# Linear recurrence layer on 128-channel tiles, with block gates that read rows of neighbouring tiles

## The chip, the cores and the metric

The kernel runs on one core of one Trainium2 chip. The metric is device time in microseconds (us) of one execution of the whole kernel, the median of several runs. The kernel computes four layers; the change concerns the second one alone, the linear recurrence layer (rglru in the code).

## The reference

A layer normalises two streams, 256 context rows and 512 latent rows of 1024 channels, applies a mixer, and adds the gated result to the streams. The mixer of the second layer is this, cut to what matters (LRU_WIDTH is 1408, in 16 blocks of 88 channels):

```python
def block_diag(x, w, b):
    xb = x.reshape(B, T, LRU_BLOCKS, LRU_BLOCK_DIM)
    return jnp.einsum('btnc,ncd->btnd', xb, w).reshape(B, T, LRU_WIDTH) + b

def rglru_coeffs(x, p, d):
    r = jax.nn.sigmoid(block_diag(x, p['gate_w'][d, 0], p['gate_b'][d, 0]))
    i = jax.nn.sigmoid(block_diag(x, p['gate_w'][d, 1], p['gate_b'][d, 1]))
    log_a = -LRU_C * r * jax.nn.softplus(-p['lam'][d])
    a = jnp.exp(log_a)
    b = jnp.sqrt(-jnp.expm1(2.0 * log_a)) * (i * x)
    return a, b

def rglru_mixer(h_l, h_c, p, ctx_out):
    def pre(h):
        z = h @ p['w_in']
        xr, g = z[..., :LRU_WIDTH], z[..., LRU_WIDTH:]
        return depthwise_conv_centred(xr, p['conv_w'], p['conv_b']), jax.nn.silu(g)
    ...
    for d in range(2):
        a, b = rglru_coeffs(x_c, p, d)
        hc, hc_final = linear_scan(a, b, h0, rev)
        a, b = rglru_coeffs(x_l, p, d)
        hl, _ = linear_scan(a, b, hc_final, rev)
    out_l = ((hs_l[0] + hs_l[1]) * g_l) @ p['w_out']
```

The gates r and i of a channel depend on the 88 channels of its own block only. Blocks of 88 do not line up with tiles of 128: 1408 is 16 blocks or 11 tiles.

## The kernel before

Channels lie on partitions and the 768 tokens (256 + 512) along the free dimension. Every product in fp32 is made of three matmuls on operands split into a rounded high part and a remainder (`split` at L224, `load_w` at L208): high by high, low by high, high by low. Each of the three is two instructions, one of 256 and one of 512 columns, which is called a pair here.

**Projections.** `dense` (L1392) makes one 128-channel tile of the input projection: 8 slices of the 1024 inputs, 24 pairs. There are 11 tiles x and 11 tiles g, in the order of L1387. A tile's weights are loaded and split one tile ahead: at slice 2 the generator calls `ahead` (L1397), which issues the DMA, the high cast (here on ScalarE and VectorE in turn, `HL`), and the subtraction of the remainder on VectorE (L221). After an x tile, `xtile` copies PSUM to `xf` on ScalarE (L1412), does the four-tap convolution on VectorE (L1415, L1417) and moves the rows by DMA into tiles of 88 channels, `xb` (L1424, L1425). After a g tile, `gtile` computes silu (L1445, L1446).

**Gates and recurrence.** `pair` (L1461) takes two blocks of 88. For each of two directions d, a key is one (block, direction), so that a pair has four. `pair_in` splits the inputs `xb` and the gate weights, VectorE and GpSimd sharing it. Each of eight gate outputs is three pairs of matmuls (L1476) and a sigmoid on ScalarE (L1480). Then ScalarE runs a burst over the four keys: four tanh (L1485), four exp (L1489), four sqrt (L1492), with table loads between. Then VectorE runs two elementwise operations (L1498, L1499) and the scan (L1501 forwards, L1504 and L1505 backwards) for each key, GpSimd adds the two directions (L1506), DMAs carry the sum from 88-channel tiles back to 128-channel tiles `zt` (L1513), VectorE multiplies by the gate g (L1517) and a DMA writes the tile to DRAM (L1519).

**Order.** `merge` (L130) interleaves two generators by weights, the projections and the pairs. ScalarE keeps the order in which the program is written (`manual_schedule`, L1530), so there an instruction waits for all that is written ahead of it. The orders of the other engines are set when the kernel is built; on the chip each engine takes its instructions in that order. After the layer, `out_proj` (L373) loads the 11 tiles back and starts its matmuls (L244).

```python
            merge(projs(), 160.0 + XP, [(pairs(), 22.0 * 8)])
```

Of the kernel before, what the change touches and what calls it, by code (L numbers as in the profile page):

```python
# [10 lines left out]
F32 = mybir.dt.float32  # L11
F32R = mybir.dt.float32r
# [137 lines left out]
class Build:  # L150
# [1195 lines left out]
    LRU_LAM, LRU_GB = 55, 87  # L1346

    def rglru(self, li, pv, md, xs, acc, xsp, last):
        tc, nc, a = self.tc, self.nc, self.a
        B = 88  # L1350
        NB = 16
        self.hi_dve = HL
        toks = [(0, TC), (TC, TL)]
        self.open(dict(h=16, xf=2, sq=2), wb=(2, 2, 2))

        lam = pv[0:B, self.LRU_LAM:self.LRU_LAM + 32]
        st = lambda n: self.gp.tile([P, 32], F32, tag=n, name=self.nm(n), bufs=1)[0:B, :]
        ab, u, s, s2, t, spl = st("sa"), st("su"), st("ss_"), st("s2"), st("st"), st("spl")
        spn = self.gp.tile([P, 32], F32, tag="spn", name=self.nm("spn"), bufs=1)[0:B, :]
# [44 lines left out]
        def xtile(m):  # L1404

            for outs in dense(m):
                yield 1.0
            xp = self.g("xf")
            for z in (0, 258, 772):
                nc.gpsimd.memset(xp[:, z:z + 2], 0.0)  # L1410
            for pt, o0, n in ((outs[0], 2, TC), (outs[1], 260, TL)):
                nc.scalar.copy(xp[:, o0:o0 + n], pt[:, :n])  # L1412
            xc = self.g("sq")
            cw = lambda j: pv[:, self.LRU_CW + j * 11 + m:self.LRU_CW + j * 11 + m + 1]
            nc.vector.tensor_scalar(xc[:, 2:772], xp[:, 0:770], cw(0), pv[:, self.LRU_CB + m:self.LRU_CB + m + 1], op0=ALU.mult, op1=ALU.add)  # L1415
            for j in range(1, 4):
                nc.vector.scalar_tensor_tensor(out=xc[:, 2:772], in0=xp[:, j:j + 770], scalar=cw(j), in1=xc[:, 2:772], op0=ALU.mult, op1=ALU.add)  # L1417
            for b in range(NB):
                lo, hi = max(m * P, b * B), min((m + 1) * P, (b + 1) * B)
                if lo >= hi:  # L1420
                    continue
                if b not in xb:
                    xb[b] = self.g("xb")
                nc.sync.dma_start(xb[b][lo - b * B:hi - b * B, 0:TC], xc[lo - m * P:hi - m * P, 2:2 + TC])  # L1424
                nc.sync.dma_start(xb[b][lo - b * B:hi - b * B, TC:T], xc[lo - m * P:hi - m * P, 260:260 + TL])  # L1425
# [34 lines left out]

        def pair(p):  # L1461

            self.mark(f"pair{p}")
            bl = (2 * p, 2 * p + 1)
            keys = [(b, d) for b in bl for d in range(2)]
# [4 lines left out]
            for gi, dstt in ((0, R), (1, I)):  # L1470
                for b, d in keys:
                    c0 = (d * 2 + gi) * B
                    outs = [self.psb(), self.psb()]
                    for p_i, (wt, xt) in enumerate(((W[b][0], X[b][0]), (W[b][1], X[b][0]), (W[b][0], X[b][1]))):
                        for pt, (s0, n) in zip(outs, SEGS):
                            nc.tensor.matmul(pt[:B, :n], wt[:B, c0:c0 + B], xt[:B, s0:s0 + n], start=(p_i == 0), stop=(p_i == 2))  # L1476
                    o = dstt[b, d] = self.g("sg")
                    cb = self.LRU_GB + (d * 2 + gi) * NB + b
                    for pt, (s0, n) in zip(outs, toks):
                        nc.scalar.activation(o[:B, s0:s0 + n], pt[:B, :n], AF.Sigmoid, bias=pv[0:B, cb:cb + 1])  # L1480
                    yield 1.0

            for b, d in keys:
                A[b, d] = self.g("aa")
                nc.scalar.activation(A[b, d][:B, :T], R[b, d][:B, :T], AF.Tanh, scale=spl[:, d * NB + b:d * NB + b + 1])  # L1485
# [440 lines left out]
```

## Time and profile before

| | |
|---|---|
| median of 3 runs | 3079.63 us (3076.31 to 3083.82) |
| the profiled execution, its own time | 3069.68 us |
| its span in the trace | 3067.8 us |
| mean granted TensorE clock in it | 0.905 |
| matmuls of the layer's projections and gates | 1056 and 384 |
| first projection matmul of the layer | 1070.61 us |
| last gate matmul starts | 1398 us |
| first matmul of the output projection | 1446.29 us |

Times in the trace are counted from the span's start. TensorE is PE, VectorE is DVE, ScalarE is ACT, GpSimd is POOL, and SP is the queue that issues the DMAs. "Idle before" is the time in which an engine had nothing running ahead of the instruction, and the releaser is what ended it. A clock of 1.00 is 2.4 GHz, 0.50 is 1.2 GHz.

### The profile page before, as it was taken

The numbers are of one execution on the slowest core, as the hardware profiler recorded it, in microseconds if no ns is written. First come the engines' busy times: TensorE is split into PE (matmuls) and PEld (weight loads), VectorE is DVE, ScalarE is ACT, GpSimd is POOL, SyncE is SP. The second block draws the span as 40 slices with busy tenths as digits, with TensorE's granted clock in tenths as the row PEclk, the third lists the DMA queues.
The fourth block names the chain that finished last, engine by engine and source line by source line (L and its number), as shares of the span: only waits on it lengthen the run. The fifth ranks groups of instructions, "written<-read, shape, count | busy, mean of one in ns | idle before, by whom it ended". The sixth has DMA issues, their size and how long they took to land. (4 is left out here: it accounts for less than half of the span.)

```text
span 3067.8 us, 66309 instructions
## 1 busy us (share of the span) xinstructions
PE 2639.3 (86%) x27760; PEld 2146.5 (70%) x27760; DVE 2009.2 (65%) x3325; ACT 1462.7 (48%) x2666; POOL 759.9 (25%) x640
## 2 busy tenths in 40 slices
PE   5999988888887988883989999998897887888887
PEld 3876777677776777762778888877684665777775
DVE  4768787697873478896334344343778777888853
ACT  3454553556553266664243443442454444656561
POOL 1013442031212034643022232220104333111211
PEclk9998899899998999895989999999797888889988
DMA  6235544444326422222731111046234545533423
GB/s 222 93 119 191 185 174 157 138 133 131 111 88 218 171 67 80 88 68 101 265 110 47 49 47 56 28 153 222 67 105 177 182 170 176 153 122 122 132 72 117
DMA packets 169552, 391.84 MB, mean 128 GB/s; under 512 B 20518, under 2 KB 52262, under 8 KB 169254
## 3 DMA queue, kind: packets, MB, share of 16 engines
q1 hardware_dynamic: 169254, 387.61, 37.9%
q8 instruction: 218, 3.57, 0.5%
q14 instruction: 80, 0.66, 0.1%
HBM read 281.24 MB, written 97.65 MB: 124 GB/s over the span
## 5 line engine op out<-in xcount | busy, mean ns | idle before, releaser
L634 PE MATMUL pa<-x,wh 128*128 128x512 f32 (+1 forms) x1552 | 408.2, 371 | 43.3 <-ACT x L227 24.0
L634 PEld LDWEIGHTS pa<-x,wh 128*128 128x128 f32 x1552 | 288.1, 202 | 98.8 <-ACT x L227 28.6
L244 PE MATMUL pa<-z,wh 128*128 128x256 f32 (+1 forms) x992 | 243.4, 357 | 62.0 <-ACT z L227 57.6
L1574 PE MATMUL pa<-h,wh 128*128 128x256 f32 (+1 forms) x1024 | 255.6, 355 | 8.0 <-ACT wh L218 7.0
L244 PEld LDWEIGHTS pa<-z,wh 128*128 128x128 f32 x992 | 173.0, 193 | 105.1 <-ACT z L227 59.0
L221 DVE TENSOR_TENSOR wl<-wr,wh 128x1024 fp32r<-128x1024 f32 (+1 forms) x148 | 190.6, 1290 | 81.2 <-ACT wh L218 80.5
L634 PE MATMUL pa<-x,wl 128*128 128x512 f32 (+1 forms) x776 | 232.5, 370 | 6.0 <-DVE wl L221 6.0
L218 ACT CAST wh<-wr 128x1024 fp32r<-128x1024 f32 (+1 forms) x137 | 146.5, 1070 | 190.9 <-PE pa L244 126.1
L912 DVE TENSOR_TENSOR tmpN<-al,N 128x31 f32<-128x31 f32 (+15 forms) x496 | 211.9, 427 | 14.0
L914 DVE TENSOR_TENSOR N<-N,tmpN 128x31 f32<-128x31 f32 (+15 forms) x496 | 210.6, 425 | 12.8
L1574 PEld LDWEIGHTS pa<-h,wh 128*128 128x128 f32 x1024 | 179.0, 194 | 45.3 <-issue 17.6
L1401 PE MATMUL pa<-h,wh 128*128 128x256 f32 x704 | 169.5, 352 | 17.2 <-DVE gt L1446 9.3
L634 PEld LDWEIGHTS pa<-x,wl 128*128 128x128 f32 x776 | 156.5, 204 | 31.4 <-DVE wl L221 7.9
L1401 PEld LDWEIGHTS pa<-h,wh 128*128 128x128 f32 x704 | 129.0, 198 | 38.5 <-issue 5.6
L407 DVE SCALAR_TENSOR_TENSOR x<-pa,md,x 128x512 f32<-128x512 f32 (+1 forms) x56 | 33.4, 632 | 167.5 <-PE pa L244 167.5
L244 PE MATMUL pa<-z,wl 128*128 128x256 f32 (+1 forms) x496 | 138.6, 351 | 0.5 <-DVE wl L221 0.5
L227 ACT CAST x<-xf 128x770 fp32r<-128x770 f32 x96 | 80.1, 835 | 123.0 <-DVE xf L528 73.6
L854 PE MATMUL A<-krs,be 64*128 64x128 f32 x1536 | 120.2, 295 | 19.6 <-ACT sc L865 8.8
L1574 PE MATMUL pa<-h,wl 128*128 128x256 f32 (+1 forms) x512 | 136.2, 346 | 0.6 <-DVE wl L221 0.6
L733 POOL TENSOR_SCALAR pcs<-pm 128x12 f32<-128x12 f32 (+2 forms) x48 | 38.4, 812 | 387.2 <-ACT pm L730 374.7
L868 DVE TENSOR_TENSOR sc<-A,msk 128x512 f32<-128x512 f32 x128 | 82.7, 685 | 74.3 <-PE A L854 74.1
L854 PEld LDWEIGHTS A<-krs,be 64*128 64x128 f32 x1536 | 101.4, 196 | 34.9 <-ACT sc L865 9.5
(329 smaller groups left out, 6592.6 us busy)
## 6 DMA issues: line engine op xcount, KB each, us to landing
wr<-in_l_win_dram SPq DMA_DIRECT2D x118, 512.0 KB
ar<-in_l_ada_dram SPq DMA_DIRECT2D x88, 512.0 KB
krd<-kr SPq DMA_DIRECT2D x32, 768.0 KB
bed<-be SPq DMA_DIRECT2D x32, 768.0 KB
krs<-krd SPq DMA_DIRECT2D x96, 256.0 KB
be<-bed SPq DMA_DIRECT2D x96, 256.0 KB
kr<-krd SPq DMA_DIRECT2D x96, 256.0 KB
uv<-vn SPq DMA_DIRECT2D x192, 64.0 KB
```

The costliest lines, as they stand in the source:

```text
L218: nc.scalar.copy(hi, raw)
L221: lo_eng.tensor_tensor(out=lo, in0=raw, in1=hi.bitcast(F32), op=ALU.subtract)
L227: nc.scalar.copy(hi, src)
L244: nc.tensor.matmul(outs[si][:mw, :n], wt[:kp, ws], xt[:kp, s0:s0 + n], start=(kt == 0 and p_i == 0), stop=(kt == nk - 1 and p_i == 2),)
L634: nc.tensor.matmul(outs[si][:, :n], wt[:, ws], xt[:, s0:s0 + n], start=(first and p_i == 0), stop=(final and p_i == 2))
L733: nc.gpsimd.tensor_scalar(pcs[:, m, o0:o0 + iv.shape[1], d], iv, 1.0, None, op0=ALU.mult)
L854: nc.tensor.matmul(T_["s"][hh][:, c * 128:c * 128 + 128].rearrange("p (s x) -> p s x", s=2), T_["be"][hs, c, :], kv, start=True, stop=True)
L868: y = op("V", 602, pr, [x], lambda h, ov2=ov2, mv=mv, iv=iv: nc.vector.tensor_tensor(out=ov2, in0=iv().rearrange("p (j q x) -> p j q x", j ...
L912: nc.vector.tensor_tensor(out=tv, in0=al[:, i + 1:32, i:i + 1].broadcast_to([P, n, w]), in1=N[:, i:i + 1, 0:w].broadcast_to([P, n, w]), op ...
L914: nc.vector.tensor_tensor(out=N[:, i + 1:32, 0:w], in0=N[:, i + 1:32, 0:w], in1=tv, op=ALU.subtract))
L1401: nc.tensor.matmul(pt[:, :n], wt[:, ws], xt[:, s0:s0 + n], start=(kt == 0 and p_i == 0), stop=(kt == KT - 1 and p_i == 2))
L1574: nc.tensor.matmul(pt[:, :n], wt[:, ws], xt[:, s0:s0 + n], start=(kt == 0 and p_i == 0), stop=(kt == KT - 1 and p_i == 2))
```

## The change

All of the layer works on 11 tiles of 128 channels. The convolved x stays in its tile `xc` (five buffers) and is split there. The gates of an output tile m are a matmul over whole 128-row sources with zero-padded weights: an odd tile reads itself and one gathered tile of the neighbours' edge rows (`halo`, moved by two DMAs and split into `ha`); an even tile reads itself and its neighbours whole. So gate outputs cost two or three times three pairs. The zero-padded weights are loaded one (tile, gate) ahead by `gw_in`. `unit` takes two tiles, four keys as before. The moves to 88-channel tiles and back are gone. All weight casts are on ScalarE, the order of the projections and the merge weights are new. Line numbers of the new kernel are about 1 to 13 higher: L1413 for the copies, L1416 and L1418 for the convolution, L1465 for the gate weights, L1486 for the gate matmuls, L1492 for the sigmoids, L1497, L1502, L1505 for tanh, exp, sqrt, L1509, L1510 for the elementwise steps, L1512, L1515, L1516 for the scans, L1518 for the sum, L1519 for the gate product.

```diff
-        B = 88
-        NB = 16
-        self.hi_dve = HL
+        NT = 11
+        HSEG = ((2, TC), (260, TL))
-        self.open(dict(h=16, xf=2, sq=2), wb=(2, 2, 2))
+        self.open(dict(h=16, xf=2, xc=5, sq="xc"), wb=(3, 2, 2))
...
         def xtile(m):
...
-            xc = self.g("sq")
+            x = xc[m] = self.g("xc")
...
-            for b in range(NB):
...
-                nc.sync.dma_start(xb[b][lo - b * B:hi - b * B, 0:TC], xc[lo - m * P:hi - m * P, 2:2 + TC])
-                nc.sync.dma_start(xb[b][lo - b * B:hi - b * B, TC:T], xc[lo - m * P:hi - m * P, 260:260 + TL])
+            hi, lo = X[m] = self.g("xh", F32R), self.g("xh", F32R)
+            self.split(x[:, 2:772], hi[:, 2:772], lo[:, 2:772])
+            if m and m % 2 == 0:
+                r1, r2 = halo(m - 1)
+                n, xf = r1 + r2, self.g("xf")
+                nc.sync.dma_start(xf[0:r1, 2:772], xc[m - 2][P - r1:P, 2:772])
+                nc.sync.dma_start(xf[r1:n, 2:772], x[0:r2, 2:772])
+                hi, lo = X["n", m - 1] = self.g("ha", F32R), self.g("ha", F32R)
+                self.split(xf[:n, 2:772], hi[:n, 2:772], lo[:n, 2:772])
...
-        self.open(dict(xb=6, zt=3, gt=4, b=4, sg=12, aa=4))
+        self.open(dict(xh=8, ha=2, gt=4, sg=12, aa=4))
...
+        def gw_in(i):
+            if i < 2 * NT:
+                m, gi = divmod(i, 2)
+                n = (base[m + 1] - base[m]) * 256
+                gr = self.wp.tile([P, 768], F32, tag="wr", name=self.nm("gr"), bufs=self.wb[0])
...
+                for s_ in range(base[m + 1] - base[m]):
+                    nc.sync.dma_start(gr[:, s_ * 256:s_ * 256 + 256], a[f"l{li}_gw"][base[m] + s_, gi])
+                self.split(gr[:, :n], gh[:, :n], gl[:, :n])
+                GW[i] = gh, gl
+        def unit(ms):
+            keys = [(m, d) for m in ms for d in range(2)]
...
+                    gh, gl = GW.pop(2 * m + gi)
+                    for d in range(2):
+                        outs = [self.psb(), self.psb()]
+                        for si, (key, k) in enumerate(srcs):
+                            ws = slice(si * 256 + d * 128, si * 256 + d * 128 + 128)
+                            for p_i, (wt, xt) in enumerate(((gh, X[key][0]), (gl, X[key][0]), (gh, X[key][1]))):
+                                for pt, (s0, n) in zip(outs, HSEG):
+                                    nc.tensor.matmul(pt[:, :n], wt[:k, ws], xt[:k, s0:s0 + n], start=(si == 0 and p_i == 0), stop=(si == len(srcs) - 1 and p_i == 2))
+                        if d == 0:
+                            gw_in(2 * m + gi + 1)
+                        o = dstt[m, d] = self.g("sg")
...
+                    z = I[m, 0]
+                    nc.gpsimd.tensor_tensor(out=z[:, :T], in0=z[:, :T], in1=hs[:, :T], op=ALU.add)
+                    nc.vector.tensor_tensor(out=z[:, :T], in0=z[:, :T], in1=gt[m][:, :T], op=ALU.mult)
+                    nc.sync.dma_start(dd, z[:, :T])
...
-            merge(projs(), 160.0 + XP, [(pairs(), 22.0 * 8)])
+            merge(projs(), 160.0, [(units(), 104.0 + 25.8) + LRF])
...
+def gate_src(m):
+    out = [(m, P)]
+    if m % 2:
+        out.append((("n", m), sum(halo(m))))
+    else:
+        out += [(q, P) for q in (m - 1, m + 1) if 0 <= q < 11]
+    return out
...
-XP = 28
+LRO = "x0 x1 x2 g0 x3 g1 x4 g2 x5 g3 x6 g4 x7 g5 x8 g6 x9 g7 x10 g8 g9 g10"
+LRF = (0.10, 1.10)
-HL = (1, 2)
```

How the instructions stand at three places. The first is ScalarE behind a burst. In the kernel before, behind the four sqrt of a pair:

```order
L1492 ACTIVATE aa_13138<-aa_13138 88x768
L1412 COPY xf_13173<-pa_13097 128x256
L1412 COPY xf_13173<-pa_13098 128x512
L218 CAST wh_13205<-wr_13203 128x1024
L1480 ACT_TABLE_LOAD
L1480 ACTIVATE sg_13301<-pb_13293,pv_87 88x256
```

Now, behind the four sqrt of the unit of tiles 2 and 3; `gh_13290` is the second gate weight of tile 4, `xf_13300` and `xc_13306` belong to x tile 6, `ha_13318` is the gathered edge of tile 5, `wh_13338` the weight of x tile 7:

```order
L1505 ACTIVATE aa_13211<-aa_13211 128x768
L227 CAST gh_13290<-gr_13289 128x768
L1492 ACT_TABLE_LOAD
L1492 ACTIVATE sg_13297<-pb_13269,pv_87 128x256
L1492 ACTIVATE sg_13297<-pb_13270,pv_87 128x512
L1413 COPY xf_13300<-pa_13167 128x256
L1413 COPY xf_13300<-pa_13168 128x512
L227 CAST xh_13311<-xc_13306 128x770
L227 CAST ha_13318<-xf_13315 48x770
L218 CAST wh_13338<-wr_13336 128x1024
L1492 ACTIVATE sg_13374<-pb_13354,pv_87 128x256
```

The casts of the convolved tile and of the gathered edge now stand on ScalarE, between the copies and the next weight cast. The second place is VectorE in the same stretch, in the new kernel, from the product of tile 2 on (nine rows of the unit's elementwise work, first L1509, stand ahead of these):

```order
L1519 TENSOR_TENSOR sg_12934<-sg_12934,gt_12894 128x768
L1512 SCALAR_TENSOR_TENSOR sg_13130<-sg_13052,aa_13201 128x768
L1509 SCALAR_TENSOR_TENSOR aa_13211<-sg_13087,aa_13211 128x768
L230 TENSOR_TENSOR glo_13291<-gr_13289,gh_13290 128x768
L1510 TENSOR_TENSOR aa_13211<-aa_13211,sg_13159 128x768
L1416 TENSOR_SCALAR xc_13306<-xf_13300,pv_87 128x770
L1515 SCALAR_TENSOR_TENSOR sg_13159<-sg_13087,aa_13211 128x256
L1418 SCALAR_TENSOR_TENSOR xc_13306<-xf_13300,pv_87,xc_13306 128x770
L1516 SCALAR_TENSOR_TENSOR sg_13159<-sg_13087,sg_13159,aa_13211 128x512
L1418 SCALAR_TENSOR_TENSOR xc_13306<-xf_13300,pv_87,xc_13306 128x770
L1519 TENSOR_TENSOR sg_13130<-sg_13130,gt_13162 128x768
L1418 SCALAR_TENSOR_TENSOR xc_13306<-xf_13300,pv_87,xc_13306 128x770
```

The convolution of x tile 6 stands among the last of the unit's elementwise work; the subtractions for `xh`, `ha` and then for the weight of x tile 7 follow it. The third place is TensorE, in the new kernel, at the first matmuls of x tile 7, ahead of which stand x tile 6, g tile 4 and three gate outputs of tile 4:

```order
L1486 MATMUL pb_13401<-xh_13020,gh_13290 128x256
L1486 MATMUL pb_13402<-xh_13020,gh_13290 128x512
L1402 MATMUL pa_13436<-h_11960,wh_13338 128x256
L1402 MATMUL pa_13437<-h_11960,wh_13338 128x512
L1486 MATMUL pb_13462<-xh_12754,gh_13290 128x256
L1486 MATMUL pb_13463<-xh_12754,gh_13290 128x512
L1402 MATMUL pa_13436<-h_11960,wl_13339 128x256
L1402 MATMUL pa_13437<-h_11960,wl_13339 128x512
```

From there the projection of x tile 7 and the rest of the unit's gates alternate, so that what waits for `wh_13338` holds up both.

## Rows read from the trace of the kernel before

**Rows 1.** The page: busy time, share of the span and instructions of each engine.
```profile
PE 2639.3 (86%) x27760; PEld 2146.5 (70%) x27760; DVE 2009.2 (65%) x3325; ACT 1462.7 (48%) x2666; POOL 759.9 (25%) x640
```

**Rows 2.** Busy time of each engine in the layer's opening, body and end.
```profile
core 0: us, PE busy (x) PEld busy (x) DVE busy (x) ACT busy (x) POOL busy (x), PEclk, DMA share, GB/s
1070.60:1105.30 34.70, 29.57 (x144) 23.42 (x144) 27.22 (x51) 17.83 (x26) 10.41 (x18) 0.93 0.23 71
1105.30:1398.80 293.50, 252.66 (x1296) 206.75 (x1296) 252.53 (x233) 188.19 (x282) 144.68 (x79) 0.90 0.24 72
1398.80:1446.30 47.50, 0.04 (x2) 0.01 (x1) 27.77 (x25) 17.00 (x20) 11.69 (x5) 0.50 0.29 104
```

**Rows 3.** Timeline of PE: start us, us, instructions, idle before and releaser.
```profile
1172.32 1.01 PE L1401 MATMUL pa<-h,wl 128*128 128x256 f32 x2 [7.23 <-DVE wl L221]
...
1176.97 1.17 PE L1401 MATMUL pa<-h,wh 128*128 128x256 f32 x4
...
1224.32 0.85 PE L1401 MATMUL pa<-h,wh 128*128 128x256 f32 x4
...
1225.35 0.86 PE L1401 MATMUL pa<-h,wh 128*128 128x256 f32 x4
...
1236.04 1.58 PE L1476 MATMUL pb<-b,gh 88*88 88x256 f32 x4 [4.73 <-POOL b L230]
...
1245.74 0.93 PE L1401 MATMUL pa<-h,wh 128*128 128x256 f32 x4
```

**Rows 4.** Timeline of ACT and of DVE around one burst.
```profile
1205.35 3.42 ACT L1485 ACTIVATE aa<-sg,spl 88x768 f32<-88x768 f32 x4
...
1217.76 0.83 ACT L1412 COPY xf<-pa 128x256 f32<-128x256 f32 x2
1218.49 1.06 ACT L218 CAST wh<-wr 128x1024 fp32r<-128x1024 f32 x1
...
1221.46 1.05 ACT L1480 ACTIVATE sg<-pb,pv 88x256 f32<-88x256 f32 x2 [0.62 <-PE pb L1476]
...
1215.68 1.82 DVE L1498 SCALAR_TENSOR_TENSOR aa<-sg,aa 88x768 f32<-88x768 f32 x2 [4.21 <-ACT aa L1492]
...
1219.16 0.67 DVE L1415 TENSOR_SCALAR sq<-xf,pv 128x770 f32<-128x770 f32 x1
1219.75 1.21 DVE L221 TENSOR_TENSOR wl<-wr,wh 128x1024 fp32r<-128x1024 f32 x1
```

**Rows 5.** Single lines of the code: duration in ns, min/median/max, first and last start.
```profile
L1498 DVE SCALAR_TENSOR_TENSOR aa<-sg,aa x32: 923/948/2593, 1132.6 to 1421.5; 88x768 f32<-88x768 f32 x32
...
L1499 DVE TENSOR_TENSOR aa<-aa,sg x32: 921/944/2542, 1135.4 to 1424.1; 88x768 f32<-88x768 f32 x32
...
L1501 DVE TENSOR_TENSOR_SCAN sg<-sg,aa x16: 1739/1744/3366, 1138.2 to 1422.4; 88x768 f32<-88x768 f32 x16
...
L1504 DVE TENSOR_TENSOR_SCAN sg<-sg,aa x16: 657/676/2262, 1139.9 to 1426.6; 88x256 f32<-88x256 f32 x16
...
L1505 DVE TENSOR_TENSOR_SCAN sg<-sg,sg,aa x16: 1268/1270/1280, 1141.3 to 1429.3; 88x512 f32<-88x512 f32 x16
...
L1506 POOL TENSOR_TENSOR sg<-sg,sg x16: 1797/3148/7552, 1142.7 to 1430.7; 88x768 f32<-88x768 f32 x16
...
L1517 DVE TENSOR_TENSOR zt<-zt,gt x11: 941/959/2603, 1161.0 to 1436.3; 128x768 f32<-128x768 f32 x11
...
L1417 DVE SCALAR_TENSOR_TENSOR sq<-xf,pv,sq x33: 986/1010/2606, 1096.6 to 1371.1; 128x770 f32<-128x770 f32 x33
```

**Rows 6.** Timeline of SP and DVE: a move of rows, and the cast behind it.
```profile
1377.55 0.81 SPq L1425 DMA_DIRECT2D xb<-sq  x1
...
1380.92 1.81 DVE L229 CAST b<-xb 88x768 fp32r<-88x768 f32 x1 [0.25 <-DMA xb<-sq]
```

**Rows 7.** Timeline of DVE and PE at the layer's end.
```profile
1436.32 0.96 DVE L1517 TENSOR_TENSOR zt<-zt,gt 128x768 f32<-128x768 f32 x1 [5.78 <-DMA zt<-sg]
...
1446.29 1.01 PE L244 MATMUL pa<-z,wh 128*128 128x256 f32 x2 [47.46 <-ACT z L227]
```

More of the change, by code (lines that the diff above doesn't have):

```diff
@@ L1386, in rglru @@
         self.pq = tc.alloc_tile_pool(name=f"lps{li}", bufs=4, space=bass.MemoryType.PSUM)
-        order = [(c[0], int(c[1:])) for c in "x0 x1 x2 g0 x3 x4 g1 g2 g3 x5 x6 g4 x7 g5 x8 g6 g7 x9 g8 x10 g9 g10".split()]
-        self.plan([(a[f"l{li}_win"][m + 11 * (c == "g")], 1024) for c, m in order])
+        order = [(c[0], int(c[1:])) for c in LRO.split()]
+        self.plan([(a[f"l{li}_win"][m + NT * (c == "g")], 1024) for c, m in order])
         self.ahead(2)
-        xb, gt, zt, zs = {}, {}, {}, []
+        xc, gt, zs = {}, {}, []
+        X = {}
         def dense(m):
@@ L1461, in pair @@
[L1461 to L1465, printed above, removed]
-            R, I, A = {}, {}, {}
-            if p == 0:
-                pair_in(0)
-            yield 1.0
[L1470 to L1485, printed above, removed]
-                (nc.gpsimd if d else nc.vector).tensor_tensor(out=I[b, d][:B, :T], in0=I[b, d][:B, :T], in1=xb[b][:B, :T], op=ALU.mult)
-                yield 0.75
-            for b, d in keys:
-                nc.scalar.activation(R[b, d][:B, :T], R[b, d][:B, :T], AF.Exp, scale=spn[:, d * NB + b:d * NB + b + 1])
-                yield 0.75
-            for b, d in keys:
-                nc.scalar.activation(A[b, d][:B, :T], A[b, d][:B, :T], AF.Sqrt)
-            yield 3.0
-            if p + 1 < NB // 2:
-                pair_in(p + 1)
-            for b, d in keys:
-                aa, bb, hs = R[b, d], A[b, d], I[b, d]
-                nc.vector.scalar_tensor_tensor(out=bb[:B, :T], in0=aa[:B, :T], scalar=1.0, in1=bb[:B, :T], op0=ALU.add, op1=ALU.mult)
-                nc.vector.tensor_tensor(out=bb[:B, :T], in0=bb[:B, :T], in1=hs[:B, :T], op=ALU.mult)
@@ L1506, in pair @@
-                    nc.gpsimd.tensor_tensor(out=I[b, 0][:B, :T], in0=I[b, 0][:B, :T], in1=hs[:B, :T], op=ALU.add)
-                    for m in range(11):
-                        lo_, hi_ = max(m * P, b * B), min((m + 1) * P, (b + 1) * B)
-                        if lo_ >= hi_:
-                            continue
-                        if m not in zt:
-                            zt[m] = self.g("zt")
-                        nc.sync.dma_start(zt[m][lo_ - m * P:hi_ - m * P, 0:T], I[b, 0][lo_ - b * B:hi_ - b * B, 0:T])
@@ L1514, in pair @@
[L1514 to L1517 removed]
+                    nc.vector.tensor_tensor_scan(out=rv(hs, TC, TL), data0=rv(aa, TC, TL), data1=rv(bb, TC, TL), initial=hs[:, 0:1], op0=ALU.mult, op1=ALU.add)
+                    z = I[m, 0]
+                    nc.gpsimd.tensor_tensor(out=z[:, :T], in0=z[:, :T], in1=hs[:, :T], op=ALU.add)
@@ L1518, in pair, with units @@
+                    nc.vector.tensor_tensor(out=z[:, :T], in0=z[:, :T], in1=gt[m][:, :T], op=ALU.mult)
                     dd = self.dp.tile([P, T], F32, tag=f"z{m}", name=self.nm("zd"))
-                    nc.sync.dma_start(dd, zt[m][:, :T])
+                    nc.sync.dma_start(dd, z[:, :T])
                     zs.append(dd)
-        def pairs():
-            for p in range(NB // 2):
-                yield from pair(p)
+                yield 0.3
+        def units():
+            for m in range(0, NT, 2):
+                yield from unit(tuple(range(m, min(m + 2, NT))))
```

101 lines of the change are left out of this document (63 added, 38 removed).

## The prediction

> **What bounds the kernel now.** I read the page first: over the whole kernel TensorE is busy 86% of the span, VectorE 65% [rows 1]. The layer concerned takes 12% of it, so I cut its stretch in three [rows 2]. It opens at 1070.6 with three projection tiles, 144 matmuls in 34.7 us. In the body (293.5 us) TensorE and VectorE are equally busy, 253 us each, at a granted clock of 0.90; neither is full, and each stops for the other. At the end TensorE is idle for 47.5 us, while the last pair's burst and scans run dry. The three are 375.7 us; that is what the change must beat.
>
> The timeline of TensorE gives its price [rows 3]. From 1224.32 to 1225.35 three pairs start, and other stretches at the same clock give the same: 0.35 us a pair, at 2.4 GHz. Behind idle times it is slower: 7 pairs in 4.65 us behind one of 7.2, and 15 pairs in 9.70 us behind one of 4.7, that is about 0.65 a pair, the 1.2 GHz level. So one stop costs 2.2 to 4.4 us beyond itself. The 720 pairs of before need 252 us at full clock.
>
> **Engine sums of the change.** Gates grow from 192 to 312 pairs: tiles 2, 4, 6 and 8 read three sources, the other seven two, 26 sources by four outputs by three pairs. With the projections' unchanged 528 that is 840 pairs, 294 us, 42 more. VectorE loses ten of 32 elementwise rounds and all casts: ten L1498 and ten L1499 are 19 us, five scans each way 18 us [rows 5]; the conversions to 88 rows and GpSimd's share of them go too. The DMAs that carried rows over and back leave SP and the waits on them; ten edge moves take their place. So by sums the layer goes from two engines equally loaded to TensorE alone, with some 42 us more on it. That alone decides nothing: what counts is whether TensorE can run through.
>
> **The path in one unit.** The orders shown above do not let it. Take t = 0 at the first tanh of the burst of tiles 2 and 3. TensorE has x tile 6, g tile 4 and three gate outputs of tile 4 ahead of x tile 7: 75 pairs, 26 us. For x tile 7 it needs a weight whose cast stands on ScalarE behind the casts of the convolved tile 6 and of its gathered edge. These wait for VectorE's convolution, and that stands late in the burst's elementwise work. Step by step:
> - Burst to VectorE's first instruction: 1215.68 less 1205.35, 10.3 us [rows 4].
> - VectorE to the end of the convolution, 21 instructions: four L1498 3.79, four L1499 3.78, two L1501 3.49, two L1504 1.35, two L1505 2.54, two products 1.92, three L1417 3.03 [rows 5]; the convolution's first step 0.67, and a gate-weight subtraction of 768 columns, by width from the 1.21 of 1024, 0.91 [rows 4]. That is 21.5; starts lie 0.08 closer than durations (0.59 against 0.67, [rows 4]), so 19.8. Twice a product waits for GpSimd's sum: 1.80 at its shortest [rows 5] less one VectorE instruction of 0.9. Together 21.6.
> - The edge rows' DMA: 1377.55 to 1380.92 for such a move, 3.4 us [rows 6].
> - Edge cast 0.8 by width, weight cast 1.06, subtraction 1.21 [rows 4]: 3.1. x tile 7 can start at 38.4, 12 to 15 us after TensorE has run out.
> - The rest of the unit on TensorE: x tile 7, three quarters of g tile 5, five gate outputs, 74 pairs, 25.9 us. Nothing else can run meanwhile, as gates and projections alternate there.
> - To the next tanh: two sigmoids 1.05, a g tile's two at the 0.83 of two copies, one weight cast 1.06 [rows 4], 0.25 to release: 3.2.
>
> The sum is 67.5 us, where 150 pairs need 52.5. The stop brings the clock down; I take the smaller price, 2.2, as part of it falls into later waiting [rows 3]. A unit takes **69.7 us**. The other units have the same stations in slightly other order.
>
> **Opening and end.** The opening: 34.7 for the first three tiles, as before, 24 pairs for g0, 102 for the first unit with its projections, 44.1, then 3.2: 82.0. At odd tile 3 a gate weight is cast behind sigmoid, copies, convolution and tile cast; by the same rows 7.2 us, less 12 matmuls beside it: 5.1. So **87.1** to the first burst. Four units follow to the fifth burst. The end: 10.3, then fourteen VectorE instructions with one wait on GpSimd and the last gate weight, 14.4; 12 pairs at 0.65, 7.8; sigmoid and release 1.3; a burst of two keys, 10.3 less 3.4 = 6.9; seven VectorE instructions 6.9; GpSimd's sum 1.8; and from the last product's start to the output projection as before, 1436.32 to 1446.29, 10.0 [rows 7]. That is **59.4**. The tail behind the last gate matmul itself shrinks (two keys for four, no move back).
>
> Sum: 87.1 + 4 x 69.7 + 59.4 = 425.3 us against 375.7: **50 us slower**. Against the profiled execution (3069.68) that is 3119; its median over the runs stands 10 us higher, so I forecast 3079.6 + 49.6 = **3129 us**.
>
> **Edits priced at nothing, and bounds.** The larger gate weights (two or three DMAs of 128 KB for each of 22) are issued one gate ahead into a ring of three; the DMA engines' share is 0.24 in the body [rows 2], and what hides them is the gate in work, 12 to 18 pairs, 4.2 to 6.3 us. Without that cover each would show as the 3.4 of a move, and only where nothing later is awaited. The high casts moved to ScalarE are 1.06 us each; ScalarE is busy 188 of 293 us [rows 2], so they cost only where I counted them. The five shared buffers at the opening are worth between a gain of the opening's own loss (34.7 less 72 pairs, 9.5 us) and nothing; I take nothing, since the splits there are as before. A VectorE instruction that meets GpSimd takes up to 2.54 for 0.94 [rows 5]: none to two a unit, 0 to 3.2; I take none, as GpSimd's splits are gone. The clock's price is 2.2 to 4.4 a unit. What I can have wrong most is overlap: every step that starts before the one ahead of it is done shortens the unit, down to 52.5.
>
> **The rivals.** *TensorE runs through (faster).* Place: the cast of the weight of the tile behind each even x tile. If VectorE, with a third fewer rounds, reaches the convolution so early that this weight is split before TensorE's 26 us are used up, a unit is 52.5 to 55. It decides at 57.3 us a unit: (375.7 - 87.1 - 59.4) / 4. At 54, with an opening of 82.0, the layer takes 357.4, 18 us less: **3061**; at 52.5, 3055. For it: VectorE is the more relieved engine, the moves are gone, and a VectorE instruction on 128 partitions takes what one on 88 does, 0.959 for 0.944 [rows 5]. Against it: the station list above has no VectorE backlog in it at all, only fixed waits. The Trainium skill (Trainium Kernel Development and Optimization, Best Practices) has "Always tile to 128 partitions" as its first rule; by that rule the change is a plain gain, and it would be this rival's time. The trace agrees that the rows are free on VectorE; the rule is silent on the padded matmuls.
>
> *No change.* The removed moves were hidden and half of my stop overlaps: a unit of 55.8 to 58.8, **3079**. For it: ScalarE has over 100 us of idle time in the body, and waits can slide.
>
> *Worse.* The odd tile stops each unit too, as in the first (5.1), and the clock takes its upper price (2.2 more): 77 us a unit, 29 us above the forecast, **3158**. Against it: in later units TensorE has 24 pairs more between the odd tile and what it needs.
>
> **How the numbers follow.** My forecast (a unit of 60 to 75 us) has 52%, the worse case 12%, no change 12%, TensorE running through 24%. A measurement of this kernel can tell about 0.2% (6 us) from no change. So slower 64%, same 12%, faster 24%. The forecast's own range is 3090 to 3150; the range of 3060 to 3158 cuts about half off each outer case, 18% in all.
>
> **What would show it.** In the new profile: bursts of tanh (L1497) some 70 us apart; on ScalarE an idle time of about 15 us ahead of the x cast (L227) behind each burst, released by the convolution L1418; on TensorE a stop of about 10 us at the projection (L1402) after each even x tile, released by the cast or subtraction of a weight, with pairs of 0.65 behind it; VectorE's share of the body well under before's. Bursts 53 to 57 us apart with TensorE idle under 5 us each would prove me wrong; a stop in another place, released by the gate weights, would leave the sign but not the reason.

## The result, and the profile after

The changed kernel takes 3120.22 us (median of 4 runs, 3116.15 to 3129.07), the kernel before took 3077.97 us beside it. The ratio is 1.0147, interval 1.0107 to 1.0186: 42 us slower. The forecast was 3129 us, 50 slower, in a range of 3060 to 3158.

The first line of the page, the busy time of each engine, answers to [rows 1]:

```profile
PE 2692.4 (86%) x28000; PEld 2195.3 (70%) x28000; DVE 1925.0 (62%) x3291; ACT 1443.0 (46%) x2638; POOL 650.1 (21%) x609
```

VectorE has 84 us less to do, GpSimd 110, ScalarE 20, and TensorE 53 more. Three engines were relieved and the kernel got slower. The busy time of the engines by stretch, cut at the first projection matmul, behind the opening's three projection tiles, at the first tanh of each burst over four keys (L1497) and at the first matmul of the output projection, answers to [rows 2]:

```profile
core 0: us, PE busy (x) PEld busy (x) DVE busy (x) ACT busy (x) POOL busy (x), PEclk, DMA share, GB/s
1073.50:1108.00 34.50, 30.64 (x146) 24.40 (x146) 27.33 (x48) 20.61 (x31) 7.97 (x13) 0.90 0.14 42
1108.00:1157.50 49.50, 49.25 (x261) 41.52 (x261) 22.29 (x28) 21.07 (x36) 3.58 (x10) 0.95 0.26 78
1157.50:1227.20 69.70, 58.85 (x305) 48.72 (x305) 38.00 (x43) 33.55 (x52) 9.69 (x13) 0.90 0.20 63
1227.20:1298.10 70.90, 58.75 (x304) 49.16 (x303) 37.70 (x42) 32.71 (x50) 8.93 (x12) 0.90 0.20 62
1298.10:1366.40 68.30, 57.58 (x296) 48.02 (x295) 37.42 (x43) 32.74 (x50) 7.47 (x11) 0.93 0.18 56
1366.40:1433.40 67.00, 58.97 (x302) 49.32 (x301) 32.71 (x39) 31.73 (x50) 8.68 (x7) 0.92 0.14 46
1433.40:1492.80 59.40, 17.34 (x75) 13.69 (x73) 28.86 (x31) 30.11 (x39) 9.45 (x7) 0.65 0.19 69
```

Read the four units of 67 to 71 us: TensorE is busy 58 to 59 us in each (part of it at the lower clock), VectorE 33 to 38, ScalarE 32 to 34. Nothing is full. The layer takes 419.4 us against 375.7, 43.7 of the profiled spans' difference of 48.6; it also starts 2.9 us later, at 1073.46 for 1070.61.

What the engines wait for in the four units (engine, line waited for, total us, times, longest):

```profile
ACT xh L227 <- DVE xc L1418: 74.9, 7, 17.7
ACT sg L1492 <- PE pb L1486: 58.6, 17, 5.4
...
PE pb L1486 <- ACT sg L1492: 20.8, 3, 9.7
...
PE pb L1486 <- DVE glo L230: 12.7, 4, 4.0
PE pa L1402 <- ACT wh L218: 8.2, 1, 8.2
```

The largest wait of ScalarE is the one the prediction named: the cast of the convolved tile waits for the convolution. It is seen at work on ScalarE's timeline in the unit of tiles 2 and 3, which answers to [rows 4] (start, duration, engine, line, then the idle time and its releaser):

```profile
1227.18 3.43 ACT L1497 ACTIVATE aa<-sg,spl 128x768 f32<-128x768 f32 x4
...
1242.68 0.86 ACT L1413 COPY xf<-pa 128x256 f32<-128x256 f32 x2
1261.02 0.83 ACT L227 CAST xh<-xc 128x770 fp32r<-128x770 f32 x1 [17.48 <-DVE xc L1418]
1263.38 0.83 ACT L227 CAST ha<-xf 48x770 fp32r<-48x770 f32 x1 [1.53 <-DMA xf<-xc]
1264.12 1.04 ACT L218 CAST wh<-wr 128x1024 fp32r<-128x1024 f32 x1
1265.07 1.04 ACT L1492 ACTIVATE sg<-pb,pv 128x256 f32<-128x256 f32 x2
```

For 17.5 us ScalarE has nothing before it but a cast that cannot start, and behind it stand the weight that TensorE needs next and the sigmoids that empty PSUM, the memory that the matmuls write to. What the cast waits for, on VectorE: the first instruction behind the burst, one of the two products that wait for GpSimd's sum, and the last step of the convolution:

```profile
1237.52 1.83 DVE L1509 SCALAR_TENSOR_TENSOR aa<-sg,aa 128x768 f32<-128x768 f32 x2 [8.96 <-ACT aa L1505]
...
1247.98 0.96 DVE L1519 TENSOR_TENSOR sg<-sg,gt 128x768 f32<-128x768 f32 x1 [1.74 <-POOL sg L1518]
...
1259.97 1.02 DVE L1418 SCALAR_TENSOR_TENSOR xc<-xf,pv,xc 128x770 f32<-128x770 f32 x1
```

TensorE's stops, from its timeline:

```profile
1186.70 1.37 PE L1486 MATMUL pb<-xh,gh 128*128 128x256 f32 x2 [9.74 <-ACT sg L1492]
...
1252.38 0.72 PE L1486 MATMUL pb<-xh,glo 128*128 128x256 f32 x2 [3.93 <-DVE glo L230]
...
1265.21 1.01 PE L1402 MATMUL pa<-h,wh 128*128 128x256 f32 x2 [8.21 <-ACT wh L218]
...
1270.23 0.52 PE L1402 MATMUL pa<-h,wl 128*128 128x256 f32 x2
...
1336.32 0.58 PE L1486 MATMUL pb<-xh,gh 128*128 128x256 f32 x1 [6.75 <-ACT sg L1492]
...
1406.21 0.48 PE L1486 MATMUL pb<-xh,gh 128*128 128x256 f32 x1 [4.29 <-ACT sg L1492]
```

Every unit has one stop that ScalarE ends; in one of the four it is at the projection (1265.21), in the others at a gate matmul whose PSUM buffer waits for a sigmoid. Behind the stop of 8.21 us come 8 pairs in 5.0 us, from 1265.21 to 1270.23, 0.63 a pair, with a granted clock of 0.54 over that stretch, near the 1.2 GHz level; at 0.35 they take 2.8, so the clock's part is 2.2 us.

### The profile page after: what moved, and what is told of

It is laid out like the page before. It is cut to its first block, busy times and chain, and to the rows that moved or that the text cites. A ratio compares the mean times of both kernels' runs of the same rounds, so it can differ in the third digit from the quotient of the medians.

```text
span 3116.4 us, 66606 instructions
## 1 busy us (share of the span) xinstructions
PE 2692.4 (86%) x28000; PEld 2195.3 (70%) x28000; DVE 1925.0 (62%) x3291; ACT 1443.0 (46%) x2638; POOL 650.1 (21%) x609
## 5 line engine op out<-in xcount | busy, mean ns | idle before, releaser
L218 ACT CAST wh<-wr 128x1024 fp32r<-128x1024 f32 (+1 forms) x148 | 158.1, 1068 | 179.9 <-PE pa L244 126.3
L634 PEld LDWEIGHTS pa<-x,wl 128*128 128x128 f32 x776 | 156.2, 204 | 31.3 <-DVE wl L221 7.8
```

What stands on the lines that cost most here:

```text
L218: nc.scalar.copy(hi, raw)
L634: nc.tensor.matmul(outs[si][:, :n], wt[:, ws], xt[:, s0:s0 + n], start=(first and p_i == 0), stop=(final and p_i == 2))
```

## The experiments

Theory A: the wait for the convolution, put into ScalarE's order by the cast, stops TensorE in every unit. Rival B: TensorE's extra pairs, or ScalarE's extra casts as work, make the time. The layer of each run, by its parts, from the traces (opening: first projection matmul to first tanh; end: fifth tanh to the first matmul of the output projection; us):

| run | opening | four units | end | layer | ratio to before |
|---|---|---|---|---|---|
| changed kernel | 84.0 | 69.7 70.9 68.3 67.0 | 59.5 | 419.4 | 1.0147 |
| 1 casts on VectorE | 77.7 | 68.4 61.6 59.7 59.4 | 57.6 | 384.4 | 1.0038 |
| 2 fewer pairs | 78.5 | 63.7 65.9 64.4 63.0 | 56.9 | 392.3 | 1.0062 |
| 3 the wait alone | 83.8 | 69.6 71.1 68.2 67.0 | 59.4 | 419.0 | 1.0126 |
| 4 late casts on ScalarE | 79.2 | 66.7 61.6 59.7 59.6 | 58.5 | 385.3 | 1.0036 |
| 6 gate remainders on GpSimd | 77.8 | 63.2 67.8 66.2 66.1 | 52.3 | 393.4 | 1.0070 |
| 7 all remainders on GpSimd | 82.8 | 61.9 64.3 63.0 67.7 | 52.6 | 392.3 | 1.0063 |
| 8 gate weights early | 78.4 | 65.1 66.0 63.1 62.6 | 52.1 | 387.3 | 1.0024 |
| 9 late casts, early weights | 79.9 | 63.4 63.9 62.0 62.4 | 52.5 | 384.1 | 1.0024 |
| 10 one remainder a unit on GpSimd | 78.4 | 60.4 62.8 62.5 62.9 | 52.7 | 379.7 | 1.0019 |
| 11 product later | 78.4 | 58.9 64.3 61.8 62.5 | 53.6 | 379.5 | 1.0033 |
| 12 the same, late casts | 79.9 | 64.6 62.3 62.9 62.8 | 52.5 | 385.0 | 1.0032 |

Run 5 is the kernel before with one wait added; its layer takes 410.7. The parts are of one profiled execution each. The rest of the kernel is the same code in every run and takes from 2687 to 2711 us in these executions, so the layer is the finer measure, and the ratio does not put runs 8 to 12 in order.

**1. The casts of x and edge rows on VectorE.**

```diff
-            self.split(x[:, 2:772], hi[:, 2:772], lo[:, 2:772])
+            self.split(x[:, 2:772], hi[:, 2:772], lo[:, 2:772], hi_eng=nc.vector)
...
-                self.split(xf[:n, 2:772], hi[:n, 2:772], lo[:n, 2:772])
+                self.split(xf[:n, 2:772], hi[:n, 2:772], lo[:n, 2:772], hi_eng=nc.vector)
```

> The high casts of the convolved x tile and of its gathered edge move from ScalarE to VectorE; matmuls and everything else stay. Theory A (ScalarE is blocked in order behind the convolution, so the next weight cast and sigmoid come late): in a unit the weight of x tile 7 is then cast at about t = 18 us after the first tanh instead of 38; what ends last is its remainder on VectorE, behind the burst's elementwise work, at about 34; 64 pairs (22.4 us) and 3.2 us follow, so a unit takes about 60 us instead of 69, some 35 us in four units, and 5 us more in the opening: about 3080 us. Theory B (the 120 added pairs, 42 us at full clock, are the loss): no change, 3120 us, or a little slower for VectorE's 16 more casts.

Measured: 3085.82 us (3079.26 to 3090.84), ratio 1.0038 [1.0019, 1.0056]. The layer gives back 35.0 of the 43.7 us. TensorE's timeline has these stops left in the same stretch:

```profile
1180.72 1.01 PE L1486 MATMUL pb<-xh,glo 128*128 128x256 f32 x2 [11.53 <-DVE glo L230]
...
1242.22 1.01 PE L1486 MATMUL pb<-xh,glo 128*128 128x256 f32 x2 [3.58 <-DVE glo L230]
...
1252.07 0.62 PE L1402 MATMUL pa<-h,wl 128*128 128x256 f32 x2 [0.74 <-DVE wl L221]
```

No stop is released by ScalarE any more. What is left is released by VectorE, the remainder of a gate weight, 11.5 us in the first unit and some 4 later. So the first unit gains only 1.3 us: this stop takes the place of one of 9.7.

**2. Fewer pairs.** In the loop over products of L1484:

```diff
-for p_i, (wt, xt) in enumerate(((gh, X[key][0]), (gl, X[key][0]), (gh, X[key][1]))):
+for p_i, (wt, xt) in enumerate(((gh, X[key][0]), (gl, X[key][0]), (gh, X[key][1]))[:3 if si == 0 else 1]):
...
-nc.tensor.matmul(pt[:, :n], wt[:k, ws], xt[:k, s0:s0 + n], start=(si == 0 and p_i == 0), stop=(si == len(srcs) - 1 and p_i == 2))
+nc.tensor.matmul(pt[:, :n], wt[:k, ws], xt[:k, s0:s0 + n], start=(si == 0 and p_i == 0), stop=(si == len(srcs) - 1 and p_i == 0))
```

> Of a gate's sources after the first (the neighbour tiles, or the gathered edge) only the product of the two high parts is computed; the two correction products of these sources are left out, so that 192 pairs of gate matmuls are left, as many as before the change; everything else stays. Theory B (the added matmuls are the loss): 42 us come back, about 3078 us. Theory A (the stop behind the x casts): only pairs on the path count, 12 of them in a unit from x tile 7 on (4.2 us), 16 in the first unit (5.6 us), 4 at the slow rate at the end (2.6 us): 25 us faster than the change, about 3095 us, with bursts about 65 us apart and the stop in each unit longer by the pairs that went ahead of it.

Measured: 3092.69 us (3090.84 to 3096.99), ratio 1.0062 [1.0042, 1.0082]. 15 sources less two products for four outputs are 120 pairs, 42 us at 0.35. The layer gains 27, and the wait stays as it was:

```profile
ACT xh L227 <- DVE xc L1418: 74.7, 7, 17.7
```

So the pairs count as well, but not all of them: the time is near A's 3095, where only those behind the stop count, and not B's 3078. TensorE's stops in the four units grow from 41.7 to 58.6 us in sum, as it reaches them earlier. Taking away all that the padding added to the gates does not bring back the old time.

**3. The wait without the work.** As run 1, and ScalarE copies two columns where it cast:

```diff
+            nc.scalar.copy(tiny[:, 0:2], x[:, 2:4])
+            self.split(x[:, 2:772], hi[:, 2:772], lo[:, 2:772], hi_eng=nc.vector)
...
+                nc.scalar.copy(tiny[:n, 0:2], xf[:n, 2:4])
+                self.split(xf[:n, 2:772], hi[:n, 2:772], lo[:n, 2:772], hi_eng=nc.vector)
```

> The run with all casts of x and edge rows on VectorE (3085.8 us) took both the work (11 + 5 casts, some 13 us) and the wait for the convolution from ScalarE. Here the casts stay on VectorE, and ScalarE only copies two columns of the convolved tile, and of the gathered edge, in the old place: under 0.2 us of work each, but the wait is back. A (the wait in ScalarE's order is the cause): bursts 66 to 71 us apart again and 3110 to 3125 us, idle time of 10 to 17 us on ScalarE ahead of these copies. B (ScalarE's work was too much): within 4 us of 3086, bursts 60 apart.

Measured: 3118.93 us (3116.55 to 3121.65), ratio 1.0126 [1.0108, 1.0144]. ScalarE's timeline in the same unit:

```profile
1246.07 0.87 ACT L1414 COPY xf<-pa 128x256 f32<-128x256 f32 x2
1264.41 0.19 ACT L1421 COPY tiny<-xc 128x2 f32<-128x2 f32 x1 [17.48 <-DVE xc L1419]
1266.80 0.19 ACT L1430 COPY tiny<-xf 48x2 f32<-48x2 f32 x1 [2.19 <-DMA xf<-xc]
1266.89 1.04 ACT L218 CAST wh<-wr 128x1024 fp32r<-128x1024 f32 x1
```

Copies of 0.19 us bring back 34.6 of the 35.0 us, every unit within 0.2 us of the changed kernel's. What the casts' work adds on ScalarE lies within the 0.4 us that is left; their wait is the price. This settles A against ScalarE's load.

**4. The same casts on the same engine, written later.** Those of an even tile and of its edge go just ahead of the odd tile's gates:

```diff
-            self.split(x[:, 2:772], hi[:, 2:772], lo[:, 2:772])
+            late.append((x[:, 2:772], hi[:, 2:772], lo[:, 2:772]))
+            if m % 2:
+                self.split(*late.pop())
...
-                self.split(xf[:n, 2:772], hi[:n, 2:772], lo[:n, 2:772])
+                late.append((xf[:n, 2:772], hi[:n, 2:772], lo[:n, 2:772]))
...
                 srcs = gate_src(m)
+                while late and (m % 2 or m == 0):
+                    self.split(*late.pop(0))
```

> All casts stay on ScalarE as in the changed kernel, but those of an even x tile and of its edge are written later, just ahead of the gates of the odd tile, so behind the casts of the next weights and several sigmoids. A (the place in ScalarE's order is the cause, not the engine): the stop at the projection goes, bursts 57 to 62 us apart, 3070 to 3092 us. B (ScalarE's load, or VectorE's convolution itself, is the cause): within 8 us of 3120.

Measured: 3088.56 us (3081.42 to 3094.8), ratio 1.0036 [1.0021, 1.0051]. ScalarE's casts in one unit:

```profile
1240.26 1.08 ACT L218 CAST wh<-wr 128x1024 fp32r<-128x1024 f32 x1
...
1255.37 1.07 ACT L218 CAST wh<-wr 128x1024 fp32r<-128x1024 f32 x1
1257.90 0.84 ACT L227 CAST xh<-xc 128x770 fp32r<-128x770 f32 x1
```

The first of these weights, that of x tile 7, is cast 18 us ahead of the tile, the tile's cast finds its data ready, and the layer takes within a microsecond what run 1 takes. It was the place in the order, not the engine.

**5. The wait put into the old kernel.** One line in the kernel before, behind the convolution:

```diff
+            nc.scalar.copy(tiny[:, 0:2], xc[:, 2:4])
             for b in range(NB):
```

> The kernel before, with one thing added: behind each convolution ScalarE copies two columns of the convolved tile, 11 copies of some 0.2 us, which is the wait alone. A (a wait for the convolution in ScalarE's order is dear wherever VectorE's convolution stands behind a burst's elementwise work): 10 to 40 us slower than before, 3090 to 3120 us, idle time on ScalarE ahead of the copies. B (it is dear only where the next weight's cast follows right behind it and the unit is two whole tiles; the old kernel casts half its weights on VectorE and its pairs are shorter): within 8 us of before.

Measured: 3113.45 us (3099.44 to 3119.78), ratio 1.0136 [1.0105, 1.0167]. The line's durations, and its idle time by releaser:

```profile
L1419 ACT COPY tiny<-sq x11: 192/192/192, 1103.2 to 1402.7; 128x2 f32<-128x2 f32 x11
...
  DVE sq L1418: 114.0, 11
```

Eleven copies, 2.1 us of work, 114 us of waiting, and the layer 35.0 us longer. What TensorE waits for ScalarE between 1105 and 1440 us:

```profile
PE pb L1478 <- ACT sg L1482: 15.1, 5, 7.1
PE pa L1402 <- ACT wh L218: 9.8, 4, 3.6
...
PE pa L1402 <- ACT sg L1482: 9.3, 1, 9.3
```

These are 34.2 us, where the kernel before has 0.3 in the same stretch. This is A. The price does not hang on whole tiles or padded matmuls: a copy of 0.19 us that reads the convolution right behind it brings it into the old kernel too. The old kernel had no such wait, as it split `xb` on VectorE and GpSimd.

**6 and 7. Remainders on GpSimd.** With run 1, first those of the gate weights, then also those of the projection weights:

```diff
-                self.split(gr[:, :n], gh[:, :n], gl[:, :n])
+                self.split(gr[:, :n], gh[:, :n], gl[:, :n], lo_eng=nc.gpsimd)
...
-            self.ready.append(self.load_w(*self.todo.pop(0)))
+            self.ready.append(self.load_w(*self.todo.pop(0), lo_eng=self.wlo))
...
-            merge(projs(), 160.0, [(units(), 104.0 + 25.8) + LRF])
+            self.wlo = nc.gpsimd; merge(projs(), 160.0, [(units(), 104.0 + 25.8) + LRF])
```

> As the run with the x casts on VectorE, and the gate weights' remainders move from VectorE to GpSimd, so that they no longer stand in the middle of the burst's elementwise work. Theory A: the wait of a gate for its remainder (4 us in a unit of the change's trace) goes, the projection's weight remainder on VectorE still comes at about 33: a unit of 57 to 60 us, 3070 to 3080 us. Theory B: 3120 us. A third way: GpSimd and VectorE slow each other, as before the change (a VectorE step of 0.94 us took up to 2.5 beside GpSimd), and this is slower than the run with the x casts alone.

> As the run before it in this list, and the remainders of the layer's projection weights move to GpSimd as well (22 subtractions of 1024 columns), so that no weight waits for VectorE's burst. Theory A: nothing but GpSimd's own speed is left between TensorE and its weights; a unit falls to 53 to 57 us and the kernel to about 3055 to 3068 us, under the kernel before the change. Theory B: 3120 us. The third way (GpSimd and VectorE slow each other): a subtraction of 1024 columns beside VectorE takes 5 us or more, weights come late again, and the time is 3080 or more.

Measured: 3096.56 us, ratio 1.0070 [1.0049, 1.0091], and 3093.84 us, 1.0063 [1.0042, 1.0084]. Both slower than run 1, the third way. Two of VectorE's groups over 1157 to 1420 us (the last figures: busy us, mean ns), run 6:

```profile
L221 DVE TENSOR_TENSOR wl<-wr,wh 128x1024 fp32r<-128x1024 f32 x15 | 23.1, 1537 | 10.9 <-ACT wh L218 10.9
...
L1512 DVE TENSOR_TENSOR_SCAN sg<-sg,aa 128x768 f32<-128x768 f32 x8 | 18.9, 2368 | 0.0
```

and run 1:

```profile
L221 DVE TENSOR_TENSOR wl<-wr,wh 128x1024 fp32r<-128x1024 f32 x14 | 17.0, 1216 | 6.1 <-ACT wh L218 6.0
...
L1512 DVE TENSOR_TENSOR_SCAN sg<-sg,aa 128x768 f32<-128x768 f32 x9 | 15.7, 1749 | 0.0
```

With the remainders on GpSimd, VectorE's other instructions became longer: 2368 for 1749 ns, 1537 for 1216. The gate's stop went and one of 9 to 11 us at the projection's `wl` came in its place; in run 7 it is at the edge rows, 6.6 to 9.5 us in the later units.

**8 and 9. The next stop.** Once ScalarE is free, TensorE stops for the gate weight whose cast stands behind the burst. The second gate weight of the next unit is written ahead of the burst, with the casts on VectorE (8) or late on ScalarE (9):

```diff
-                        if d == 0:
+                        if d == 0 and not (gi == 0 and m == ms[0] and m):
                             gw_in(2 * m + gi + 1)
...
+            gw_in(2 * ms[-1] + 3)
             for m, d in keys:
                 A[m, d] = self.g("aa")
```

> Casts on VectorE as in the 3085.8 us run, and the second gate weight of the next unit is cast and subtracted ahead of the burst of tanh instead of behind it. A (with the ScalarE wait gone, the next stop is the gate weight's remainder, which stands behind the burst: 11.5 us in the first unit, 3.6 in the others, and the clock behind them): bursts 54 to 58 us apart, 3058 to 3070 us, faster than before. B (VectorE as a whole is the bound by then): bursts 60 apart and 3080 to 3090 us, the stop only in another place.

> The late casts on ScalarE and the gate weight ahead of the burst together. A: both stops gone, VectorE without the casts, bursts 53 to 57 us apart, 3055 to 3068 us, the best of all. B (VectorE's load or the gates' own waits bound it): no better than either edit alone, 3075 or more.

Measured: 3082.78 us (3078.88 to 3099.08), ratio 1.0024 [1.0008, 1.004], and 3085.53 us (3073.14 to 3091.5), 1.0024 [1.0006, 1.0043]. B in both. TensorE's timeline in run 8:

```profile
1257.89 1.01 PE L1402 MATMUL pa<-h,wl 128*128 128x256 f32 x2 [7.78 <-DVE wl L221]
...
1324.85 1.01 PE L1402 MATMUL pa<-h,wl 128*128 128x256 f32 x2 [7.89 <-DVE wl L221]
```

The stop for the gate weight is gone and one for a projection weight, of the same engine's making, stands in its place. The four units are longer in sum than in run 1 (256.7 for 249.1), the end is 5.5 us shorter.

**10, 11 and 12.** That one remainder a unit on GpSimd (10); with it the product by g one key later (11); and that with the late casts on ScalarE (12):

```diff
-        self.plan([(a[f"l{li}_win"][m + NT * (c == "g")], 1024) for c, m in order])
+        self.plan([(a[f"l{li}_win"][m + NT * (c == "g")], 1024) + ((nc.gpsimd,) if c == "x" and m in (5, 7, 9) else ()) for c, m in order])
...
-                    nc.vector.tensor_tensor(out=z[:, :T], in0=z[:, :T], in1=gt[m][:, :T], op=ALU.mult)
...
+                    prod.append((m, z))
+                if prod and d == 0:
+                    fin()
```

> As the run with the gate weights ahead of the burst (3082.8 us), whose only stop was 6 to 8 us at the projection of each odd x tile, released by the remainder of its weight, which stood on VectorE behind the burst's elementwise work, 35 us after the tanh. Here this one remainder a unit (x tiles 5, 7, 9) is on GpSimd. A (VectorE's order is the last block): it is ready some 20 us after the tanh, the stop goes, bursts 55 to 59 us apart, 3055 to 3072 us. B (the convolved tile, its edge and the gate weights are as late on VectorE, and TensorE stops for one of these instead): bursts 60 or more apart, 3076 to 3086 us.

> The same, and the product by the gate g, which makes VectorE wait 1.7 us for GpSimd's sum twice a unit, is written one key later. A (VectorE's waits in order count): 3 to 4 us less a unit than without it, 3050 to 3066 us. B (VectorE is not on the path any more): the same as without it, within 4 us.

> The same edits with the casts of x and edge rows on ScalarE, late, in place of VectorE. A (VectorE's load counts): as fast or up to 8 us faster than with VectorE's casts, 3048 to 3062 us. B (ScalarE waits for the convolution again, in another place): slower than it by 4 us or more.

Measured: 3084.25 us, ratio 1.0019 [1.0004, 1.0033]; 3083.58 us, 1.0033 [1.0021, 1.0045]; 3085.22 us, 1.0032 [1.0015, 1.0049]. B in the first two. In the third the profiled layer is 5.5 us longer than in run 11 and the median 1.6, which leaves that question open. Timelines of GpSimd, VectorE and TensorE in run 10, in the unit whose tanh starts at 1211.18:

```profile
1227.90 2.56 POOL L221 TENSOR_TENSOR wl<-wr,wh 128x1024 fp32r<-128x1024 f32 x1 [17.63 <-ACT wh L218]
1231.68 2.40 POOL L1519 TENSOR_TENSOR sg<-sg,sg 128x768 f32<-128x768 f32 x1 [1.22 <-DVE sg L1517]
...
1228.11 3.42 DVE L1517 TENSOR_TENSOR_SCAN sg<-sg,sg,aa 128x512 f32<-128x512 f32 x1
...
1232.31 2.59 DVE L1510 SCALAR_TENSOR_TENSOR aa<-sg,aa 128x768 f32<-128x768 f32 x1
...
1246.78 0.62 PE L1486 MATMUL pb<-xh,glo 128*128 128x256 f32 x2 [1.35 <-DVE glo L230]
1251.84 1.01 PE L1486 MATMUL pb<-ha,gh 48*128 48x256 f32 x2 [4.09 <-DVE ha L229]
```

The weight is ready 19.3 us after the tanh, as meant, and the stop at the projection is gone from this unit (the first and the last of the four keep one of 2.7 and 6.3 us, for a remainder that is still on VectorE). TensorE now stops for a gate weight's remainder, 35.6 us after the tanh, and for the edge rows, 40.7 us after it; these are cast behind the same convolution. Moving one item ahead of the burst's elementwise work moves the stop to the next item behind it. No version beat the kernel before; the shortest layer, run 11's, is 3.8 us longer than its 375.7. Not tried: the convolution itself ahead of the burst's elementwise work on VectorE, a burst of two keys, and fewer pairs together with run 1. The new order of the projections, the new merge weights and the weight casts that left VectorE came with the change, and no run takes them apart.

## Why the prediction was right, point by point

- **What bounds it.** Right, shown by runs 1, 3 and 4: the cast's wait in ScalarE's order is 35 of the layer's 43.7 us, and no engine is full. The padded pairs taken away alone are worth 27 (run 2), so the two shares overlap and cannot be added.
- **The stations of one unit**, in the unit at 1227.18. Burst to VectorE's first instruction: 10.3, as forecast. To the end of the convolution 23.5 for 21.6: GpSimd's sums take 2.4 us here for the 1.80 assumed, so that the two products wait 1.74 and 1.69 us for 0.9 each. Edge rows to their cast 2.4 for 3.4. From there to TensorE's start 1.8 for 3.1, since the matmul waited for the weight's cast only; the low part comes later in the order. TensorE resumes at 38.0 for 38.4; that these three misses nearly cancel is luck. From there to the next tanh 32.9, where 25.9, 3.2 and the clock's 2.2 are 31.3. The make-up of this last part was wrong. TensorE does not pause in it: it takes some 83 pairs where the forecast has 74 and a wait of 3.2. Ahead of the stop it had taken only 68 for the 75, as it had stopped there for a gate weight's remainder (3.93 us) and taken 7 pairs behind that in 4.1 us, so the clock's price in the unit is 1.7 and 2.2 us for the one 2.2. That a wait which was not there and a second stop with its slow pairs come to nearly the same is luck too.
- **The units.** 69.7, 70.9, 68.3 and 67.0 us, 275.9 for the forecast 278.8. Each unit held one stop behind the cast, as forecast, but three of four times at a gate matmul (released by a sigmoid) and not at the projection. The step said that the weight behind the cast is what TensorE misses first; all that stands behind a blocked instruction is late, and TensorE stops at whichever it needs first.
- **Opening.** 84.0 for 87.1. Both parts were off: without the wait it is 77.7 (run 1) for the 82.0 assumed, and the wait costs 6.3 for the 5.1.
- **End.** 59.5 for 59.4, with luck: to the last burst 32.7 for 33.8, and from there 26.8 for 25.6.
- **Layer.** 419.4 for 425.3, so 43.7 us longer for 49.6; the medians differ by 42.3. The opening was 3.1 too high and the units 2.9.
- **TensorE runs through.** Its condition did not hold, and run 1 shows that more was against it than the cast: with that gone the last three units still take 59 to 62 us, above the break-even of 57.3. In them TensorE stops for 3.6 to 4.0 us for a gate weight's remainder, which stands on VectorE behind the burst and which the station list left out; and it is busy 55.6 to 57.1 us with 147 to 152 pairs, 3 to 4 us more than 0.35 each. The Trainium skill (Trainium Kernel Development and Optimization, Best Practices) has "Always tile to 128 partitions"; read as a plain gain, as the prediction tried, that rule would have made this rival come true. The trace does not bear that reading out, with a kernel 1.5% slower. The rows are free on VectorE, where L1509 on 128 partitions takes 946 ns on average in the four units and L1498 on 88 takes 948 at the median [rows 5], but what the tiling freed was not on the path, and the change put a wait there.
- **No change.** The waits did not slide: the last three units hold 17.5 to 17.7 us of idle time each ahead of the x cast, and none comes near 58.8 us.
- **The edits priced at nothing.** ScalarE's extra casts as work are free (runs 3 and 4). The larger gate weights are free only under cover: their remainder stops TensorE for some 4 us in three units, ahead of the longer stop; that the end of the unit does not move by it is argued from TensorE's order, not shown by a run. Without the longer stop they are what is left (run 1). VectorE beside GpSimd, taken at none, was right: 1.3 us in the four units together.
- **Worse.** The odd tile's own wait is 4.1 us in the later units (the x cast at 1286.46), and TensorE does not stop for it.

## What to carry to other kernels

An instruction moved to an engine that has time to spare takes its waits along, and all that stands behind it in that engine's order waits too; so ask of each moved instruction when its input is ready and what is written behind it, before asking what it costs. A copy of two columns in its place measures that wait without the work, in the new kernel and in the old one. When one stop is taken away, look for the next item behind the same busy engine: here, in each of runs 1, 4 and 6 to 12, the longest stop left in each of the last three units is one that VectorE ends.

## What the runs showed of the hardware

In these traces a VectorE instruction that starts beside one of GpSimd often lasts until about the time when GpSimd is done, plus its own length. In the body of the kernel before [rows 2], 45 VectorE instructions take over 0.25 us longer than the shortest of their line and shape, 62 us in all, and beside every one of them GpSimd was at work. One of them:

```profile
1189.92 2.40 POOL L1506 TENSOR_TENSOR sg<-sg,sg 88x768 f32<-88x768 f32 x1 [9.93 <-DVE sg L1505]
...
1190.55 2.59 DVE L1498 SCALAR_TENSOR_TENSOR aa<-sg,aa 88x768 f32<-88x768 f32 x1
```

It is 1.67 us longer than the shortest (0.92), beside the 1.77 that GpSimd still had to run. So about a quarter of the 253 us for which VectorE seemed as busy as TensorE was no work of its own, and much of the 84 us that the change takes off it is this: in the four units of the changed kernel there are three such instructions, 1.3 us in all.

Moving work back to GpSimd brings it back. Between 1157 and 1420 us run 1 has 6 of these, 4.7 us, and run 6 has 24, 26.8 us. In run 10 the weight's remainder runs on GpSimd from 1227.90 for 2.56 us, and the scan that VectorE starts at 1228.11 takes 3.42 us where it takes 1.27 otherwise [rows 5]. The Trainium skill (SBUF — State Buffer, Who interferes with whom) says that a VectorE instruction with two SBUF inputs contends with a GpSimd instruction that reads SBUF, since its second input comes through the shared read interface, and that the shared pair of ports is an exclusive lock. The trace agrees, with the 2.15 us that the scan is longer beside the 2.35 that GpSimd still had to run.
